# Queries of the memory heads: a fourth column group in other heads' input products, kept in memory until they are used

## The chip, the cores and the metric

The kernel runs on one core of a Trainium2 chip. Times are device microseconds (us) of one execution. Several runs of the same program were timed; the profile is of one further execution, with the hardware profiler attached. In the tables of the profile PE is the matrix engine (PEld its weight loads), DVE the vector engine, ACT the scalar engine, POOL the general engine, and SP the engine that only issues transfers here.

## The reference

Two decoder layers over 1024 tokens of width 1024, in float32. Each layer normalises its input, multiplies it with one wide input matrix, cuts the columns into branches, and adds the product of the gated branch outputs with an output matrix. Both layers have a branch that reads 256 memory tokens with 4 heads of width 128:

```python
def memory_cross_attention(q, mem, mem_g, w_mem_kv, q_g, k_g):
    mk, mv = jnp.split(rms_norm(mem, mem_g) @ w_mem_kv, 2, axis=-1)
    q = rms_norm(q.reshape(bsz, seq, X_HEADS, X_DIM), q_g)
    mk = rms_norm(mk.reshape(bsz, m, X_HEADS, X_DIM), k_g)
    s = jnp.einsum('bshd,bmhd->bhsm', q, mk).astype(jnp.float32) * (X_DIM ** -0.5)
    p = jax.nn.softmax(s, axis=-1).astype(mv.dtype)
    o = jnp.einsum('bhsm,bmhd->bshd', p, mv)
...
proj = u @ w_in
aq, ak, av, az, bh, bc, bb, bz, xq, xz = jnp.split(proj, cuts, axis=-1)
yx = memory_cross_attention(xq, mem, mem_g, w_mem_kv, x_qn, x_kn)
y = jnp.concatenate([ya * silu(az), yb * silu(bz), yx * silu(xz)], axis=-1)
return h + y @ w_out
```

Layer 0 has, beside it, differential attention (8 heads) and a short gated convolution; layer 1 has forgetting attention (12 heads). The change concerns `xq`, the queries of the memory heads: 512 columns of the input product in each layer.

## The kernel before

The normalised input `u` lies on chip, transposed, as a high and a low part. Every large product is made of three: high times high, high times low, low times high. Two kinds of product use it.

- `token_unit` (L213) takes eight blocks of 128 tokens, one after the other. For one block it makes 8 x 3 = 24 matmuls (L224 to L226); the token block is the stationary operand and the weight columns (`wqh`, `wql`) are the moving one, so the width of the moving operand is the number of weight columns. A head's query, key and value columns are one unit 384 wide (`qkv_unit`, L480; 396 wide for the first head of layer 1, with the forget columns).
- `feature_unit` (L242) has 128 weight columns stationary and 512 tokens moving, in two halves of 24 matmuls each (L257 to L259). It makes the gates (`gate_unit`, L264) and the convolution's parts.

After a block of a token unit, `post` copies the product out of its PSUM bank on ACT (`evac`, L283), and `qk_norm` (L288) normalises it: squares on ACT into a scratch tile `sq` (L292), sums on DVE (L294), a power on POOL (`rstd`, L119 to L124), and a multiplication on DVE (L297). After every second block, two blocks later, `qk_transpose` (L300) turns the queries and keys on PE in a bank of their own.

The order of the program is head by head: the head's token unit, its gates, its attention, and in layer 0 half of a convolution group. Behind the last head come the two pairs of memory heads, `x_pair` (L614) for pair 0 and pair 1. A pair loads the keys and values of the memory from `xm` (L622, written near the start of the kernel), makes a token unit of its own for the queries of both heads, 256 wide (L630), makes two gates (`xgate`, L636), and runs the attention of both heads, alternating between them over four groups of 256 tokens (L641 to L644, `x_attend` L646). Pair 1 also starts to load the output matrix (`out_early`, L752). The output product follows (`out_proj`, L791).

A planner (the Tile framework) turns this program into one fixed instruction stream for each engine, and each engine works through its stream in order. The planner may issue a later part of the program before an earlier one: blocks under `high_priority` go ahead of others where they are ready, attention (4000) and the evacuation of products (8000) among them. So the token unit of the next head runs on PE between the matmuls of the attention of the one before. What holds the planner back, beside data, is buffers. Each tile is asked for by a tag with a fixed number of buffers. Those that matter here:

- `d`, 3 PSUM banks: products of token units, of gates and of the convolution, the transposes of L303, and most of the output product
- `y`, 2 buffers: results of an attention group (L476, L560), and in layer 0 also the squares `osq` of its normalisation (L563)
- `E2`, 2 buffers: scratch of the attention, and the two `xgate` tiles of a pair
- `hs`, 3 buffers: `th` of the gates (L279) and the memory tiles `xr` (L621), among others
- `qr`, 4 buffers 384 or 396 wide, and `sq`, 1 buffer: only for the evacuation and its squares
- `yr`, 4 buffers 512 wide: only for the loads of the output product (L774)

Of the kernel before, what the change touches and what calls it, by code (L numbers as in the profile page):

```python
# [7 lines left out]
F32 = mybir.dt.float32  # L8
# [7 lines left out]
P = 128  # L16
# [17 lines left out]
class Trunk:  # L34
    def __init__(self, ctx, tc, io):
        self.tc, self.nc, self.io = tc, tc.nc, io
        nc = self.nc
        self.const = ctx.enter_context(tc.tile_pool(name="const", bufs=1))
        self.up = ctx.enter_context(tc.tile_pool(name="up", bufs=1))
        self.pa = ctx.enter_context(tc.tile_pool(name="pa", bufs=1))  # L40
        self.pk = ctx.enter_context(tc.tile_pool(name="pk", bufs=1))
        self.st = ctx.enter_context(tc.tile_pool(name="st", bufs=4))
        self.ps = ctx.enter_context(tc.tile_pool(name="ps", bufs=2, space=PSUM))
        self.dr = ctx.enter_context(tc.tile_pool(name="dr", bufs=1, space=DRAM))

# [16 lines left out]
        self.wq_n, self.e1b, self.ptb = 384, 3, 2  # L62

# [133 lines left out]
    def unit_weights(self, w, groups, lo_eng=None, ahead=None):  # L197

        nc = self.nc
        n = sum(c for _, c in groups)  # L200
        wh, wl, raws = ahead or ([], [], {})
        per = 2 if 2 * n <= 512 else 1
        for k0 in range(len(wh), KC, per):
            raw = raws[k0] if k0 in raws else self.raw_columns(w, groups, k0, per)
            for i in range(per):
                hi = self.pw.tile([P, self.wq_n], F32R, name="wqh", tag="wqh", bufs=8)
                lo = self.pw.tile([P, self.wq_n], F32R, name="wql", tag="wql", bufs=8)
                self.split(hi[:, :n], lo[:, :n], raw[:, i, :], lo_eng[(k0 + i) % len(lo_eng)] if lo_eng else nc.gpsimd)
                wh.append(hi[:, :n])
                wl.append(lo[:, :n])  # L210
        return wh, wl
# [65 lines left out]
    def gate_half(self, out, ps):  # L277
# [3 lines left out]
        nc.vector.scalar_tensor_tensor(out=out, in0=th, scalar=1.0, in1=ps, op0=ALU.add, op1=ALU.mult)  # L281

    def evac(self, ps, n):  # L283
        raw = self.p1.tile([P, self.wq_n], F32, name="qr", tag="qr", bufs=4)
        self.nc.scalar.activation(out=raw[:, :n], in_=ps[:, :n], func=AF.Copy)  # L285
        return raw

    def qk_norm(self, x, ng, gs):  # L288

        nc = self.nc  # L290
        sq = self.p1.tile([P, 256], F32, name="sq", tag="sq", bufs=1)
        nc.scalar.activation(out=sq, in_=x[:, :256], func=AF.Square, scale=float(gs) ** -0.5)  # L292
# [74 lines left out]
    def mem_kv(self, layer, um, w):  # L367
# [111 lines left out]

    def qkv_unit(self, w, cols, ng, gs, g, extra=None, pairs=False, weights=None):  # L480
        nc = self.nc
# [16 lines left out]
        if weights is None:  # L498
            weights = self.unit_weights(w, [(c, P) for c in cols] + ([] if extra is None else [extra[0]]), None if extra is None else (nc.vector, nc.gpsimd),
                                        None if extra is None else self.ahead)  # L500
        self.token_unit(weights, self.u_lhs(0), self.u_lhs(1), NB, post)
        return (qh, ql), (kh, kd, kl, kz) if pairs else (kh, kl), *[(lambda kb, v=v: v[kb // 4][:, kb % 4 * P:(kb % 4 + 1) * P]) for v in (vh, vl)]


# [16 lines left out]
    def diff_head(self, h, w, weights=None, between=None):  # L521
        qt, kt, vh, vl = self.qkv_unit(w, self.diff_cols(h), 4, 64, self.g_a, pairs=True, weights=weights)

# [89 lines left out]

    def x_pair(self, layer, pr, w, cq, cz, w_out):  # L614
        nc = self.nc
        q0h, q0l, q1h, q1l = self.att_tiles("qh", "ql", "kh", "kl")
        qns, mem = [], []
        g = self.g_x[layer]
# [6 lines left out]

        def post(tb, ps):
            qns.append(self.qk_norm(self.evac(ps, 256), 2, P))
# [69 lines left out]
    def fox_head(self, h, w):  # L697
        nc = self.nc
        extra = None
        if h == 0:  # L700
# [4 lines left out]
            extra = ((6144, 12), post_f)  # L705
        q, k, vh, vl = self.qkv_unit(w, [h * P, 1536 + h * P, 3072 + h * P], 2, P, self.g_c, extra)
        gate = self.gate_unit(w, 4608 + h * P)
# [132 lines left out]
    def run(self, out):  # L840
        nc, tc, io = self.nc, self.tc, self.io
        mem = io["mem"][0]
        with tc.tile_pool(name="p1_0", bufs=1, reuse_waits="tile") as self.p1, tc.tile_pool(name="pw_0", bufs=1, reuse_waits="tile") as self.pw:
# [37 lines left out]
            for pr in range(2):  # L881
                self.x_pair(0, pr, w, 6144, 6656, io["e_w_out"][0])
        self.out_proj(0, io["e_w_out"][0], io["x"][0], self.h_dr, io["o_norm_g"],
                      lambda: self.weights_ahead(io["o_w_in"][0], [(c, P) for c in (0, 1536, 3072)] + [(6144, 12)]))
        with tc.tile_pool(name="pw_1", bufs=1, reuse_waits="tile") as self.pw, tc.tile_pool(name="p1_1", bufs=1, reuse_waits="tile") as self.p1:
            self.wq_n, self.e1b, self.ptb = 396, 3, 3
            w = io["o_w_in"][0]
# [3 lines left out]
            for pr in range(2):  # L891
                self.x_pair(1, pr, w, 6156, 6668, io["o_w_out"][0])
        self.out_proj(1, io["o_w_out"][0], self.h_dr, out, None)
# [31 lines left out]
```

## Time and profile before

| | |
|---|---|
| three timed runs, median | 2206.74 us (2204.52 to 2206.93) |
| the profiled execution, its own time | 2204.26 us |
| its span, from the first to the last instruction | 2202.2 us |
| mean granted clock of PE | 0.996 |
| DVE busy | 1240.5 us (56% of the span) |
| ACT busy | 1053.2 us (48%) |
| POOL busy | 1020.3 us (46%) |
| transfers | 182.99 MB, mean 83 GB/s |

The busy time of PE is a sum of matmuls that overlap, with modelled ends, so what one matmul costs is read from the distance between starts in a stretch without gaps. Rows of a timeline have the start in the span, the duration, the engine, the line, the operation, and output from input with shapes. Rows of the windows have, for a stretch, its length and then for each engine the busy time in it with the number of instructions in brackets; then come the granted clock, the share of the transfer engines and GB/s. Rows of the groups have the count, busy time, mean duration of one in ns, and the idle time of the engine just before.

### The profile page before, as it was taken

What the parts mean: (1) busy time and instruction counts of PE and PEld (TensorE: products, weight loads), DVE (VectorE), ACT (ScalarE), POOL (GpSimd) and SP (SyncE); (2) the same over time, 40 slices, a digit from 0 to 9 for tenths busy, and PEclk for the clock granted to TensorE, in tenths of its full rate; (3) what the DMA queues carried; (4) which work ended last, traced back from release to release, by engine and by line L of the source; (5) the groups of instructions that cost most, each with busy time, mean ns of one, the idle gap of its engine ahead of it and who ended that gap; (6) DMA issues with size and microseconds to landing.
All of it is one profiled execution on the core that took longest, in us unless ns stands there. A gap on an engine that the chain in (4) does not pass through costs nothing.

```text
span 2202.2 us, 35113 instructions
## 1 busy us (share of the span) xinstructions
PE 2167.8 (98%) x12528; PEld 1968.7 (89%) x12528; DVE 1240.5 (56%) x2864; ACT 1053.2 (48%) x2503; POOL 1020.3 (46%) x1352
## 2 busy tenths in 40 slices
PE   8999999999999999999999999999999999999999
PEld 7889889899898899778889999999999999998887
DVE  5656756665674677654445554554545555566532
ACT  6656455464554555433334444444444444455321
POOL 5565555555555454342334555544555554522100
PEclk9999999999999999999999999999999999999999
DMA  5450210211202112387521222201122220223743
GB/s 163 138 156 19 62 52 19 73 34 47 61 29 58 37 54 88 116 270 216 187 63 35 58 58 59 63 23 53 48 56 68 58 62 25 65 73 113 232 132 102
DMA packets 216983, 182.99 MB, mean 83 GB/s; under 512 B 19516, under 2 KB 174300, under 8 KB 216808
## 3 DMA queue, kind: packets, MB, share of 16 engines
q1 hardware_dynamic: 193768, 138.80, 21.6%
q10 hardware_dynamic: 23040, 41.95, 6.2%
q8 instruction: 98, 1.61, 0.3%
q14 instruction: 77, 0.63, 0.1%
HBM read 153.32 MB, written 27.38 MB: 82 GB/s over the span
## 4 chain that ended last, share of the span: by engine, by line
PE 91%; DMA 4%; DVE 1%; POOL 1%; ACT 1%; issue 1%; SPq 0%; ACTq 0%; POOLq 0%; DVEq 0%
PE pd L225 11%; PE pd L224 11%; PE pd L226 11%; PE pss L417 8%; PE pd L258 7%; PE pd L257 7%; PE pd L259 7%; PE pd L788 5%; PE pd L786 5%; PE pd L787 5%; PE pt L451 4%; PE po L466 2%; PE po L465 2%; PE po L464 2%; PE pt L306 1%; DMA wraw<-in_e_w_out_dram 1%
## 5 line engine op out<-in xcount | busy, mean ns | idle before, releaser
L224 PE MATMUL pd<-wqh,u 128*128 128x384 f32 (+2 forms) x1504 | 502.2, 335 | 0.7 <-ACT u L130 0.7
L225 PE MATMUL pd<-wql,u 128*128 128x384 f32 (+2 forms) x1504 | 500.8, 333 | 0.1
L226 PE MATMUL pd<-wqh,u 128*128 128x384 f32 (+2 forms) x1504 | 500.8, 333 | 0.0
L225 PEld LDWEIGHTS pd<-wql,u 128*128 128x128 f32 x1504 | 284.2, 189 | 5.8 <-DVE wql L131 0.6
L224 PEld LDWEIGHTS pd<-wqh,u 128*128 128x128 f32 x1504 | 284.1, 189 | 4.8 <-ACT u L130 1.1
L226 PEld LDWEIGHTS pd<-wqh,u 128*128 128x128 f32 x1504 | 283.7, 189 | 4.7 <-DVE u L131 0.2
L257 PE MATMUL pd<-u,wfh 128*128 128x512 f32 x704 | 279.0, 397 | 0.0
L258 PE MATMUL pd<-u,wfl 128*128 128x512 f32 x704 | 278.7, 396 | 0.0
L259 PE MATMUL pd<-u,wfh 128*128 128x512 f32 x704 | 277.8, 395 | 0.0
L131 POOL TENSOR_TENSOR wql<-raw,wqh 128x384 fp32r<-128x384 f32 (+2 forms) x214 | 210.2, 998 | 78.2 <-ACT wqh L130 73.5
L285 ACT ACTIVATE qr<-pd 128x384 f32<-128x384 f32 (+2 forms) x200 | 92.9, 468 | 199.4 <-PE pd L226 198.4
L131 DVE TENSOR_TENSOR yl<-yr,yh 128x512 fp32r<-128x512 f32 x128 | 103.7, 810 | 142.3 <-ACT yh L130 134.2
L124 POOL TENSOR_TENSOR rs_r<-rs_v,neghalf 128x2 f32<-128x2 f32 (+2 forms) x220 | 176.4, 802 | 12.8
L130 ACT ACTIVATE yh<-yr 128x512 fp32r<-128x512 f32 x128 | 80.5, 630 | 207.8 <-PE pd L787 113.4
L130 ACT ACTIVATE pth<-pt 128x512 fp32r<-128x512 f32 (+1 forms) x232 | 121.8, 554 | 112.5 <-PE pt L451 107.4
L131 POOL TENSOR_TENSOR vl<-qr,vh 128x128 fp32r<-128x128 f32 x160 | 79.0, 499 | 206.4 <-ACT vh L130 205.5
L723 POOL TENSOR_TENSOR fbias<-ck,cqn 128x896 f32<-128x896 f32 (+3 forms) x96 | 112.4, 1171 | 131.8 <-DVE mx L434 109.1
L297 DVE TENSOR_TENSOR qr<-qr,rs_r 128x256 f32<-128x256 f32 x200 | 123.5, 618 | 79.8 <-POOL rs_r L124 78.6
L131 POOL TENSOR_TENSOR wfl<-rawf,wfh 128x512 fp32r<-128x512 f32 x88 | 119.6, 1362 | 102.7 <-ACT wfh L130 100.2
L130 ACT ACTIVATE wqh<-raw 128x384 fp32r<-128x384 f32 (+2 forms) x252 | 114.7, 483 | 109.5 <-DMA raw<-in_e_w_in_dram 61.2
L131 DVE TENSOR_TENSOR ptl<-pt,pth 128x512 fp32r<-128x512 f32 (+1 forms) x232 | 143.8, 639 | 34.6 <-ACT pth L130 32.2
L259 PEld LDWEIGHTS pd<-u,wfh 128*128 128x128 f32 x704 | 132.7, 188 | 27.1 <-issue 1.1
(286 smaller groups left out, 5077.5 us busy)
## 6 DMA issues: line engine op xcount, KB each, us to landing
yr<-y_dr ACTq DMA_DIRECT2D x128, 256.0 KB
raw<-in_o_w_in_dram SPq DMA_DIRECT2D x96, 192.0 KB
rawf<-in_e_w_in_dram SPq DMA_DIRECT2D x56, 256.0 KB
y_dr<-y SPq DMA_DIRECT2D x112, 128.0 KB
raw<-in_e_w_in_dram SPq DMA_DIRECT2D x64, 192.0 KB
wraw<-in_e_w_out_dram SPq DMA_DIRECT2D x32, 256.0 KB
rn<-on_dr ACTq DMA_DIRECT2D x32, 256.0 KB
rawf<-in_o_w_in_dram SPq DMA_DIRECT2D x32, 256.0 KB
```

What stands on the lines that cost most here:

```text
L124: nc.gpsimd.tensor_tensor(out=r[:, :n], in0=v[:, :n], in1=self.neghalf[:, :n], op=ALU.pow)
L130: nc.scalar.activation(out=hi, in_=src, func=AF.Copy)
L131: lo_eng.tensor_tensor(out=lo, in0=src, in1=f32(hi), op=ALU.subtract)
L224: nc.tensor.matmul(ps[:, :n], lhsT=ah(k), rhs=h, start=(k == 0), stop=False)
L225: nc.tensor.matmul(ps[:, :n], lhsT=ah(k), rhs=l, start=False, stop=False)
L226: mm = nc.tensor.matmul(ps[:, :n], lhsT=al(k), rhs=h, start=False, stop=(k == KC - 1))
L257: nc.tensor.matmul(ps, lhsT=h, rhs=uh[:, k, :], start=(k == 0), stop=False)
L258: nc.tensor.matmul(ps, lhsT=l, rhs=uh[:, k, :], start=False, stop=False)
L259: nc.tensor.matmul(ps, lhsT=h, rhs=ul[:, k, :], start=False, stop=(k == KC - 1))
L297: nc.vector.tensor_tensor(out=v, in0=v, in1=r.unsqueeze(2).broadcast_to([P, ng, gs]), op=ALU.mult)
L417: nc.tensor.matmul(ps, lhsT=q[qb // 4][rows, qs], rhs=k[c0 // 512][rows, ks], start=(i == 0), stop=(i == n - 1))
L723: nc.gpsimd.tensor_tensor(out=b[:, :kext], in0=ck[:, :kext], in1=self.cqn[:, qb, h:h + 1].broadcast_to([P, kext]), op=ALU.subtract)
```

## The change

The token unit of `x_pair` is gone. Of each layer, the heads 2 to 5 get a fourth group of 128 weight columns in their token unit, the query columns of memory head 0 to 3, so that these eight units are 512 wide and not 384. The wider block is copied out of PSUM, its last 128 columns are sent to memory (`xq_dr`) by a transfer that ACT issues, and `x_pair` loads the queries of its two heads back, two token blocks to a tile, normalises them, and transposes them, before it makes its gates. The weight tiles are 512 wide for all units. The evacuated blocks, and the tiles into which `x_pair` loads, are buffers of tag `yr`, shared with the output product; tags `qr` and `sq` are gone. The squares of a token unit go into the first 256 columns of the unit's own PSUM bank, already copied out; the squares of `x_pair` go into buffers of tag `y`. The code of `x_pair` up to its gates is traced in program order without a raised priority, where the `post` of the token unit had one.

```diff
+        self.xq_dr = [[self.dr.tile([NB, P, 2, P], F32, name=f"xq_dr{i}_{j}") for j in range(2)] for i in range(2)]
...
-                hi = self.pw.tile([P, self.wq_n], F32R, name="wqh", tag="wqh", bufs=8)
-                lo = self.pw.tile([P, self.wq_n], F32R, name="wql", tag="wql", bufs=8)
+                hi = self.pw.tile([P, 512], F32R, name="wqh", tag="wqh", bufs=8)
+                lo = self.pw.tile([P, 512], F32R, name="wql", tag="wql", bufs=8)
...
+    def evac_tile(self):
+        return self.pk.tile([P, 512], F32, name="qr", tag="yr", bufs=4)
+
     def evac(self, ps, n):
-        raw = self.p1.tile([P, self.wq_n], F32, name="qr", tag="qr", bufs=4)
+        raw = self.evac_tile()
...
-    def qk_norm(self, x, ng, gs):
-        sq = self.p1.tile([P, 256], F32, name="sq", tag="sq", bufs=1)
+    def qk_norm(self, x, ng, gs, ps=None):
+        sq = self.pa.tile([P, 256], F32, name="sq", tag="y", bufs=2) if ps is None else ps[:, :256]
...
         def post(tb, ps):
-            raw = self.evac(ps, 384 if extra is None else 396)
-            qns.append(self.qk_norm(raw, ng, gs))
+            raw = self.evac(ps, n)
+            if xq is not None:
+                layer, head = xq[0]
+                nc.scalar.dma_start(out=self.xq_dr[layer][head // 2][tb, :, head % 2, :], in_=raw[:, 384:])
+            qns.append(self.qk_norm(raw, ng, gs, ps))
...
+    def xq_cols(layer, h, c0):
+        return ((layer, h - 2), c0 + (h - 2) * P) if 2 <= h < 6 else None
...
-        def post(tb, ps):
-            qns.append(self.qk_norm(self.evac(ps, 256), 2, P))
-            if tb % 2:
-                self.later(DEFER, lambda: self.qk_transpose(qns[tb - 1:tb + 1], [(q0h, q0l, g), (q1h, q1l, g)], (tb - 1) * P))
-        self.token_unit(self.unit_weights(w, [(cq + pr * 256, 256)]), self.u_lhs(0), self.u_lhs(1), NB, post)
+        for tb in range(0, NB, 2):
+            t = self.evac_tile()
+            nc.sync.dma_start(out=t.rearrange("p (b c) -> p b c", b=2), in_=self.xq_dr[layer][pr][tb:tb + 2].rearrange("b p s c -> p b (s c)"))
+            qns = [self.qk_norm(t[:, i * 256:(i + 1) * 256], 2, P) for i in range(2)]
+            self.qk_transpose(qns, [(q0h, q0l, g), (q1h, q1l, g)], tb * P)
```

More of the change, by code (lines that the diff above doesn't have):

```diff
@@ L61, in __init__ @@
         self.attb, self.gorder = 3, (3, 2, 1, 0)
-        self.wq_n, self.e1b, self.ptb = 384, 3, 2
+        self.e1b, self.ptb = 3, 2
     def params(self, first):
@@ L388, in post_k @@
             def post_k(b, ps, pr=pr, qns=qns):
-                qns.append(self.qk_norm(self.evac(ps, 256), 2, P))
+                qns.append(self.qk_norm(self.evac(ps, 256), 2, P, ps))
                 if b == 1:
@@ L478, in gated_y, with qkv_unit @@
         self.emit_y(layer, chunk, 2 * g, y)
-    def qkv_unit(self, w, cols, ng, gs, g, extra=None, pairs=False, weights=None):
+    def qkv_unit(self, w, cols, ng, gs, g, extra=None, pairs=False, weights=None, xq=None):
         nc = self.nc
@@ L498, in qkv_unit @@
         if weights is None:
-            weights = self.unit_weights(w, [(c, P) for c in cols] + ([] if extra is None else [extra[0]]), None if extra is None else (nc.vector, nc.gpsimd),
+            weights = self.unit_weights(w, [(c, P) for c in cols] + ([] if extra is None else [extra[0]]) + ([] if xq is None else [(xq[1], P)]), None if extra is None else (nc.vector, nc.gpsimd),
                                         None if extra is None else self.ahead)
+        n = weights[0][0].shape[1]
         self.token_unit(weights, self.u_lhs(0), self.u_lhs(1), NB, post)
         return (qh, ql), (kh, kd, kl, kz) if pairs else (kh, kl), *[(lambda kb, v=v: v[kb // 4][:, kb % 4 * P:(kb % 4 + 1) * P]) for v in (vh, vl)]
+    @staticmethod
+    def xq_cols(layer, h, c0):
+        return ((layer, h - 2), c0 + (h - 2) * P) if 2 <= h < 6 else None
     def lam_setup(self):
@@ L521, in diff_head @@
     def diff_head(self, h, w, weights=None, between=None):
-        qt, kt, vh, vl = self.qkv_unit(w, self.diff_cols(h), 4, 64, self.g_a, pairs=True, weights=weights)
+        qt, kt, vh, vl = self.qkv_unit(w, self.diff_cols(h), 4, 64, self.g_a, pairs=True, weights=weights, xq=self.xq_cols(0, h, 6144))
         full = slice(0, P)
@@ L611, in conv_group, with x_pair @@
         yield
-    def x_pair(self, layer, pr, w, cq, cz, w_out):
+    def x_pair(self, layer, pr, w, cz, w_out):
         nc = self.nc
         q0h, q0l, q1h, q1l = self.att_tiles("qh", "ql", "kh", "kl")
-        qns, mem = [], []
+        mem = []
         g = self.g_x[layer]
@@ L624, in x_pair @@
             mem.append((xh, xl))
-        def post(tb, ps):
-            qns.append(self.qk_norm(self.evac(ps, 256), 2, P))
-            if tb % 2:
-                self.later(DEFER, lambda: self.qk_transpose(qns[tb - 1:tb + 1], [(q0h, q0l, g), (q1h, q1l, g)], (tb - 1) * P))
-        self.token_unit(self.unit_weights(w, [(cq + pr * 256, 256)]), self.u_lhs(0), self.u_lhs(1), NB, post)
+        for tb in range(0, NB, 2):
[3 more added lines that the diff above has]
+            self.qk_transpose(qns, [(q0h, q0l, g), (q1h, q1l, g)], tb * P)
         heads = []
@@ L705, in fox_head @@
             extra = ((6144, 12), post_f)
-        q, k, vh, vl = self.qkv_unit(w, [h * P, 1536 + h * P, 3072 + h * P], 2, P, self.g_c, extra)
+        q, k, vh, vl = self.qkv_unit(w, [h * P, 1536 + h * P, 3072 + h * P], 2, P, self.g_c, extra, xq=self.xq_cols(1, h, 6156))
         gate = self.gate_unit(w, 4608 + h * P)
@@ L881, in run @@
             for pr in range(2):
-                self.x_pair(0, pr, w, 6144, 6656, io["e_w_out"][0])
+                self.x_pair(0, pr, w, 6656, io["e_w_out"][0])
         self.out_proj(0, io["e_w_out"][0], io["x"][0], self.h_dr, io["o_norm_g"],
@@ L885, in run @@
         with tc.tile_pool(name="pw_1", bufs=1, reuse_waits="tile") as self.pw, tc.tile_pool(name="p1_1", bufs=1, reuse_waits="tile") as self.p1:
-            self.wq_n, self.e1b, self.ptb = 396, 3, 3
+            self.e1b, self.ptb = 3, 3
             w = io["o_w_in"][0]
@@ L891, in run @@
             for pr in range(2):
-                self.x_pair(1, pr, w, 6156, 6668, io["o_w_out"][0])
+                self.x_pair(1, pr, w, 6668, io["o_w_out"][0])
         self.out_proj(1, io["o_w_out"][0], self.h_dr, out, None)
```

## The prediction

> **What bounds the kernel now.** I read the page first, engines and chain of waits, and then windows over the two stretches in which the memory heads run: from the first 256-wide product of pair 0 to the last gate product of pair 1 in layer 0, and from the last gate of head 11 to the same point in layer 1.
>
> ```profile
> span 2202.2 us, 35113 instructions
> PE 2167.8 (98%) x12528; PEld 1968.7 (89%) x12528; DVE 1240.5 (56%) x2864; ACT 1053.2 (48%) x2503; POOL 1020.3 (46%) x1352
> PE 91%; DMA 4%; DVE 1%; POOL 1%; ACT 1%; issue 1%; SPq 0%; ACTq 0%; POOLq 0%; DVEq 0%
> ...
> 783.40:910.00 126.60, 126.48 (x911) 118.37 (x910) 85.88 (x236) 70.24 (x194) 49.53 (x65) 1.00 0.21 62
> 1879.50:2017.00 137.50, 137.50 (x965) 127.73 (x964) 92.78 (x245) 74.61 (x193) 49.24 (x68) 1.00 0.20 59
> ```
>
> PE sets the end: 91% of the chain is matmuls. In the memory heads' stretches too it never rests (126.48 of 126.60 us, 137.50 of 137.50). DVE, the third busy time of a window's row, works 68% of them (85.88 of 126.6; 92.78 of 137.5). So the question is twofold: how much PE work the change removes in all, and whether PE stays without gaps in these stretches when work is taken out of them.
>
> **The products: what PE gains.** The price of a matmul is the distance of starts in a gapless stretch. These are the first and last of 8 matmuls 256 wide, of 23 that are 384 wide, and of 16 with 512 moving columns.
>
> ```profile
> 794.06 0.28 PE L224 MATMUL pd<-wqh,u 128*128 128x256 f32 x1
> 794.89 0.28 PE L225 MATMUL pd<-wql,u 128*128 128x256 f32 x1
> ...
> 1478.01 0.34 PE L225 MATMUL pd<-wql,u 128*128 128x384 f32 x1
> 1481.89 0.34 PE L226 MATMUL pd<-wqh,u 128*128 128x384 f32 x1
> ...
> 838.45 0.39 PE L257 MATMUL pd<-u,wfh 128*128 128x512 f32 x1
> 841.85 0.39 PE L257 MATMUL pd<-u,wfh 128*128 128x512 f32 x1
> ```
>
> That is 0.83/7 = 0.1186 us, 3.88/22 = 0.1764 us and 3.40/15 = 0.2267 us. Removed: 4 units x 8 blocks x 24 = 768 matmuls, 91.1 us. Added: 8 units x 8 x 24 = 1536 matmuls that get 0.0503 us longer, 77.3 us. Net 13.8 us of 2204, because fewer matmuls carry the same columns. The Trainium skill (TensorE: Matmul & The Clock Gate, Back-to-back issue gap) speaks against even that: it gives N/2.4 + 2.5 ns for a warm stream, which at these widths would make 83.8 us removed and 81.9 added, 1.9 us net. The three distances here lie up to 14 ns above that formula, and the measured ones decide.
>
> The 77.3 us go into heads where PE is the chain, so they are paid in full. The 91.1 us come out of the two stretches, 45.5 us each, and are won only as far as something else doesn't take their place.
>
> **What holds the rest of the stretch.** Buffers of one tag seem to be handed out in the order in which the code asks for them, not as they come free. Witness the memory tiles `xr` (tag `hs`): the code asks for them right after the `th` tiles of the gates before.
>
> ```profile
> 141.72 0.91 SPq L383 DMA_DIRECT2D xm<-mkt  x2
> ...
> 1815.55 0.60 ACT L280 ACTIVATE th<-pd 128x512 f32<-128x512 f32 x1 [2.09 <-PE pd L259]
> 1879.27 0.94 SPq L622 DMA_DIRECT2D xr<-xm  x2
> 1879.55 0.60 ACT L280 ACTIVATE th<-pd 128x512 f32<-128x512 f32 x1 [2.09 <-PE pd L259]
> ...
> 849.14 0.99 SPq L622 DMA_DIRECT2D xr<-xm  x2
> 851.68 0.58 ACT L280 ACTIVATE th<-pd 128x512 f32<-128x512 f32 x1
> ```
>
> Their data is in memory from 142 us on. They are loaded at 849 and 1879 us, within 3 us of the last `th` asked for before them, although the three `hs` buffers stood nearly empty before. Read so, the change ties two knots. The squares of `x_pair` now ask for `y`, behind every `y` and `osq` of the attention before: pair 0 can't normalise until the last head's attention is at its last group, pair 1 until pair 0's is. And the four transposes of `x_pair` ask for banks of tag `d` ahead of its gates, so the gate products, the only other PE work of a pair, wait for the eighth normalised block. The removed token unit was what PE did meanwhile; its own squares had a buffer to themselves.
>
> So each layer's stretch becomes a chain of six steps. Their rows: the last `y` of the head before, the last gate of pair 0, its second and eighth result, in layer 0 and then in layer 1.
>
> ```profile
> 848.21 0.48 DVE L561 SCALAR_TENSOR_TENSOR y<-po,g_o,gate 128x256 f32<-128x256 f32 x1 [2.36 <-PE po L466]
> 852.41 0.68 DVE L281 SCALAR_TENSOR_TENSOR xgate<-th,pd 128x512 f32<-128x512 f32 x1
> 862.29 0.41 DVE L477 SCALAR_TENSOR_TENSOR y<-po,xgate 128x256 f32<-128x256 f32 x1
> 883.06 0.42 DVE L477 SCALAR_TENSOR_TENSOR y<-po,xgate 128x256 f32<-128x256 f32 x1
> ...
> 1937.23 0.42 DVE L477 SCALAR_TENSOR_TENSOR y<-po,gate 128x256 f32<-128x256 f32 x1 [0.25 <-PE po L466]
> 1953.63 0.41 DVE L477 SCALAR_TENSOR_TENSOR y<-po,xgate 128x256 f32<-128x256 f32 x1
> 1975.91 0.41 DVE L477 SCALAR_TENSOR_TENSOR y<-po,xgate 128x256 f32<-128x256 f32 x1
> ...
> 783.40:848.70 65.30, 65.18 (x461) 60.31 (x460) 42.99 (x118) 36.45 (x99) 31.25 (x40) 1.00 0.19 55
> 1880.20:1937.70 57.50, 57.50 (x417) 54.12 (x417) 37.27 (x104) 30.15 (x76) 27.69 (x41) 1.00 0.19 52
> ```
>
> ```profile
> L124 POOL TENSOR_TENSOR rs_r<-rs_v,neghalf 128x2 f32<-128x2 f32 x136 | 98.4, 724 | 6.3
> L122 POOL TENSOR_SCALAR rs_v<-qk_ms 128x2 f32<-128x2 f32 x136 | 34.0, 250 | 139.6 <-DVE qk_ms L294 131.9
> L294 DVE TENSOR_REDUCE qk_ms<-sq 128x2 f32<-128x256 f32 x136 | 56.7, 417 | 99.3 <-ACT sq L292 98.3
> L297 DVE TENSOR_TENSOR qr<-qr,rs_r 128x256 f32<-128x256 f32 x8 | 3.6, 448 | 5.0 <-POOL rs_r L124 5.0
> L314 DVE SCALAR_TENSOR_TENSOR ql<-pt,g_c,qh 128x256 fp32r<-128x256 f32 x48 | 23.0, 478 | 19.0 <-ACT qh L313 18.8
> L654 DVE TENSOR_REDUCE nm<-pss 128x1 f32<-128x256 f32 x64 | 25.9, 418 | 11.3 <-PE pss L417 11.0
> L659 DVE TENSOR_SCALAR ex<-ex,rl 128x256 f32<-128x256 f32 x64 | 23.5, 370 | 1.9
> L658 DVE RECIPROCAL rl<-ls 128x1 f32<-128x1 f32 x64 | 10.1, 159 | 12.9 <-ACT ex L656 12.2
> L131 DVE TENSOR_TENSOR ptl<-pt,pth 128x512 fp32r<-128x512 f32 x152 | 101.2, 685 | 17.0 <-ACT pth L130 14.9
> ```
>
> 1. The rest of the last head's attention took 65.3 and 57.5 us beside token unit and gates, with DVE busy 43.0 and 37.3. Of that, norms and their transposes are 8 x (0.417 + 0.448 + 0.478) = 10.7 us, gates 3 and 2 x 0.68, and early memory-head softmaxes 7 and 4 x (0.418 + 0.370 + 0.159): 19 and 16 us that aren't this attention's. It keeps 24 and 21 us on DVE, the lower ends; the old lengths are the upper. DVE was 66% busy then; with PE out of its way I take 72%: 33 and 30 us.
> 2. Eight norms, paced by POOL: 8 x (0.250 + 0.724) = 7.8 us, and some 2 us for the first square and the last multiplication and transposes: 10 us. Nothing runs on PE but transposes.
> 3. The four gate halves: 96 x 0.2267 = 21.8 us, with about 5 us of the pair's first scores, transposes and products between: 27 us.
> 4. The second head's first result needs the fourth half, and there is one `po` bank; six results follow. They took 20.8 and 22.3 us with other work on DVE; DVE's own share is 6 x (0.685 + 0.42) and some 6 softmaxes of 0.947, 12.3 us. I take 17.
> 5. The norms of pair 1: 10 us again.
> 6. Its gates: 27 us.
>
> Layer 0: 33 + 10 + 27 + 17 + 10 + 27 = 124 us against 126.6; layer 1: 30 + 91 = 121 against 137.5. About 19 us are recovered of the 91.1.
>
> **What else it costs.** PE will have gaps of many us, and the trace shows what follows one: after a window with PE 1.59 of 4 us busy the granted clock is 0.50 for two windows.
>
> ```profile
> 916.00:920.00 4.00, 1.59 (x10) 1.11 (x8) 2.58 (x3) 2.57 (x5) 2.55 (x2) 0.96 0.63 201
> 920.00:924.00 4.00, 2.14 (x8) 1.88 (x9) 1.86 (x5) 1.57 (x3) 0.71 (x1) 0.50 0.78 273
> 924.00:928.00 4.00, 3.07 (x12) 2.08 (x10) 3.35 (x4) 2.32 (x5) 4.00 (x4) 0.50 0.93 243
> ```
>
> Four gate stages restart after such a gap; each loses between nothing and 4 us (8 us at half clock). I take 2 us in all, since transposes come before the gates. The Trainium skill (TensorE: Matmul & The Clock Gate, Part 1) has half clock after an idle window of about 3.4 us and full clock after 3.4 busy ones; by it the four would lose 7 us.
>
> At nothing I cost: the 64 transfers out and 16 in (4.2 MB each way, transfers 20% busy here; the stores sit on ACT's queue, the loads on SP's behind `y` stores, and pair 0's can go while the last head still runs); the wider evacuation, split and weight loads, under PE's 24 x 0.2267 = 5.4 us per block; and the squares in the bank, which hold it about 0.8 us longer (one square and one sum), covered by the next block's 24 x 0.1764 = 4.2 us. If that cover fails, 160 blocks x 0.8 = 128 us would be the end, but two more banks stand ready, and I take 0. A gain is excluded there, as PE didn't wait for `d`. After the last gate, `u` comes free and the output product starts in the same order as before.
>
> **The sum.** 2204.3 + 77.3 - 19 + 2 = 2265 us for the profiled execution; the median of the runs shown lies 2.5 us above its own time, so some 2268.
>
> **The rivals.** *The gates run ahead* (buffers are not handed out in order, or the planner finds other work). Then steps 2 and 5 vanish behind gates, and DVE's 85.9 and 92.8 us at 85% set the stretches: 101 and 109 us, 54 us recovered, 2204.3 + 77.3 - 53.6 + 2.5 = 2230. For it: the old order of attention and products was mixed finely everywhere. Against it: the `xr` loads. *PE stays the bound*, the other side: if also DVE's work packs so that PE has under 6.9 us of gaps per layer, the 13.8 us come through: 2193. For it: DVE 68% busy. Against it: what is left for PE is 126.6 - 45.5 = 81 and 92 us, and DVE alone needs 86 and 93. By the formula of the skill above this rival would end at 2205, no change. *The tail doesn't shrink*: step 1 keeps its old length, because the fixed streams make the attention wait as it does now: up to 32 and 26 us more, towards 2325.
>
> **Chances.** Forecast 0.60; gates ahead 0.17; PE the bound 0.12 (with it 0.03 for no change); tail kept 0.08. The range leaves out the two cases at or below no change (0.15) and the far end of the last (0.05): 2213 to 2300. A measurement here can tell about 0.2%, 4.4 us, from no change. Faster 0.12, same 0.03, slower 0.85.
>
> **What would show it.** Right: eight units of 512-wide products at 0.227 us; PE gaps of 10 us and more before each pair's gates, with the clock at 0.5 in them; squares of `x_pair` only after the last `y` or `osq`; gate products only after the fourth pair of transposes. Wrong: gate products of a pair between matmuls of the attention before it, or an unbroken PE in the stretches.

## The result and the profile after

| | before | after |
|---|---|---|
| median | 2205.01 us (2203.34 to 2206.93, 6 runs) | 2304.85 us (2303.35 to 2308.69, 6 runs) |
| ratio to before | 1 | 1.0455, 95% interval 1.0444 to 1.0465 |
| profiled execution | 2204.26 us, span 2202.2 | 2307.14 us, span 2305.1 |
| mean granted clock | 0.996 | 0.975 |

The change makes the kernel 100 us slower. The forecast was 2268 us, 63 slower; the range ended at 2300. The direction was right, the size was not.

These are lines of the page of after: busy times, PE's busy tenths and granted clock in 40 slices, and the chain by engine.

```profile
PE 2211.8 (96%) x11760; PEld 1921.3 (83%) x11760; DVE 1234.7 (54%) x2864; ACT 1048.1 (45%) x2439; POOL 1008.9 (44%) x1320
PE   8999999999999988899999999999999999889999
PEclk9999999999999998799999999999999999988999
PE 82%; DMA 5%; DVE 4%; POOL 4%; ACT 3%; issue 2%; SPq 0%; ACTq 0%; POOLq 0%; DVEq 0%
```

Two things stand there. PE has 768 matmuls fewer and is still busy 44 us longer (2211.8 against 2167.8), though the forecast had it 14 us lighter. And it now has gaps: in slices 15 to 17 and 35 to 36 of 57.6 us each, which hold the memory heads' stretches, it falls to 8 tenths, and its clock to 7 or 8 in slices 16 and 17, 36 and 37. Its share of the chain went from 91 to 82%.

The windows over these stretches say how large the gaps are. First the two rows of before, from the first 256-wide product of pair 0 (in layer 1 from the last gate of head 11) to the last gate product of pair 1; then those of after between the same points, the start of layer 0's moved by the shift of the heads ahead of it. Length, PE, PEld, DVE, ACT, POOL, then the clock.

```profile
783.40:916.76 133.36, 133.24 (x946) 124.18 (x945) 90.88 (x246) 75.50 (x206) 53.01 (x68) 1.00 0.22 65
1880.20:2014.90 134.70, 134.70 (x948) 125.28 (x948) 90.95 (x244) 72.77 (x190) 47.55 (x67) 1.00 0.19 58
```

```profile
831.00:975.43 144.43, 113.39 (x560) 92.39 (x559) 89.30 (x236) 67.29 (x174) 49.43 (x61) 0.80 0.21 63
1987.00:2116.18 129.18, 105.54 (x544) 86.96 (x543) 84.38 (x228) 61.88 (x155) 43.94 (x59) 0.87 0.23 66
```

PE has 386 and 404 instructions fewer there, yet layer 0's stretch is 11 us longer and layer 1's only 5.5 us shorter. PE rests 31 and 24 us there, and runs at 0.80 and 0.87 of its clock. All that was taken out of the stretches is given back.

The shift of the heads comes from the last gates of head 7 and head 11, in before (first fence) and in after.

```profile
764.26 0.69 DVE L281 SCALAR_TENSOR_TENSOR gate<-th,pd 128x512 f32<-128x512 f32 x1
1880.18 0.69 DVE L281 SCALAR_TENSOR_TENSOR gate<-th,pd 128x512 f32<-128x512 f32 x1 [4.18 <-ACT th L280]
```

```profile
811.68 0.69 DVE L282 SCALAR_TENSOR_TENSOR gate<-th,pd 128x512 f32<-128x512 f32 x1
1986.98 0.68 DVE L282 SCALAR_TENSOR_TENSOR gate<-th,pd 128x512 f32<-128x512 f32 x1
```

Layer 0's heads are late by 47.4 us at the end of the last, where 38.6 were forecast, half of 77.3. By the end of layer 1's heads it is 106.8.

The last rows of after are the knots themselves, a timeline of the stretch, layer 0 and then layer 1: the last `y` of the head before, the first square of `x_pair`, the first and last gate product of pair 0, its last `y`, and the first and last gate product of pair 1.

```profile
871.75 0.48 DVE L575 SCALAR_TENSOR_TENSOR y<-po,g_o,gate 128x256 f32<-128x256 f32 x1 [2.31 <-PE po L471]
874.09 0.42 ACT L297 ACTIVATE sq<-qr 128x256 f32<-128x256 f32 x1 [0.94 <-DMA y_dr<-y]
887.77 0.40 PE L258 MATMUL pd<-u,wfh 128*128 128x512 f32 x1
916.11 0.40 PE L260 MATMUL pd<-u,wfh 128*128 128x512 f32 x1
932.50 0.42 DVE L482 SCALAR_TENSOR_TENSOR y<-po,xgate 128x256 f32<-128x256 f32 x1 [1.80 <-PE po L471]
946.01 0.77 PE L258 MATMUL pd<-u,wfh 128*128 128x512 f32 x1
947.43 0.63 PE L258 MATMUL pd<-u,wfh 128*128 128x512 f32 x1
948.66 0.39 PE L258 MATMUL pd<-u,wfh 128*128 128x512 f32 x1
975.43 0.40 PE L260 MATMUL pd<-u,wfh 128*128 128x512 f32 x1
...
2015.17 0.42 DVE L482 SCALAR_TENSOR_TENSOR y<-po,gate 128x256 f32<-128x256 f32 x1 [0.76 <-PE po L471]
2028.48 0.78 PE L258 MATMUL pd<-u,wfh 128*128 128x512 f32 x1
2058.67 0.39 PE L260 MATMUL pd<-u,wfh 128*128 128x512 f32 x1
2073.41 0.42 DVE L482 SCALAR_TENSOR_TENSOR y<-po,xgate 128x256 f32<-128x256 f32 x1 [1.14 <-PE po L471]
2087.39 0.78 PE L258 MATMUL pd<-u,wfh 128*128 128x512 f32 x1
2116.18 0.39 PE L260 MATMUL pd<-u,wfh 128*128 128x512 f32 x1
```

Read it downwards: `y`, square, gates, `y`, gates, in strict turns. The square names what it waited for, `DMA y_dr<-y`: its buffer comes free when the transfer that sends the last `y` away has landed.

### The profile page after: what moved, and what is told of

It reads as the page before. It is cut to its first block, busy times and chain, and to the rows that moved or that the text cites. A ratio compares the mean times of both kernels' runs of the same rounds, so it can differ in the third digit from the quotient of the medians.

```text
span 2305.1 us, 33833 instructions
## 1 busy us (share of the span) xinstructions
PE 2211.8 (96%) x11760; PEld 1921.3 (83%) x11760; DVE 1234.7 (54%) x2864; ACT 1048.1 (45%) x2439; POOL 1008.9 (44%) x1320
## 4 chain that ended last, share of the span: by engine, by line
PE 82%; DMA 5%; DVE 4%; POOL 4%; ACT 3%; issue 2%; SPq 0%; ACTq 0%; POOLq 0%; DVEq 0%
PE pd L226 11%; PE pd L225 11%; PE pd L227 11%; PE pss L422 6%; PE pd L258 6%; PE pd L259 6%; PE pd L260 5%; PE pd L802 4%; PE pd L800 4%; PE pd L801 4%; PE pt L456 4%; PE po L471 2%; PE po L470 2%; PE po L469 2%; DMA raw<-in_e_w_in_dram 2%
## 5 line engine op out<-in xcount | busy, mean ns | idle before, releaser
L225 PE MATMUL pd<-wqh,u 128*128 128x384 f32 (+2 forms) x1248 | 458.0, 368 | 1.5 <-ACT u L131 0.9
L226 PE MATMUL pd<-wql,u 128*128 128x384 f32 (+2 forms) x1248 | 457.5, 367 | 0.1
L227 PE MATMUL pd<-wqh,u 128*128 128x384 f32 (+2 forms) x1248 | 456.5, 366 | 0.0
L225 PEld LDWEIGHTS pd<-wqh,u 128*128 128x128 f32 x1248 | 235.8, 189 | 24.6 <-ACT u L131 1.4
L226 PEld LDWEIGHTS pd<-wql,u 128*128 128x128 f32 x1248 | 235.8, 189 | 22.8 <-DVE wql L132 0.6
L227 PEld LDWEIGHTS pd<-wqh,u 128*128 128x128 f32 x1248 | 235.5, 189 | 22.9 <-DVE u L132 0.2
L132 POOL TENSOR_TENSOR wql<-raw,wqh 128x384 fp32r<-128x384 f32 (+3 forms) x182 | 203.3, 1131 | 87.7 <-ACT wqh L131 78.6
L290 ACT ACTIVATE qr<-pd 128x384 f32<-128x384 f32 (+3 forms) x168 | 87.5, 524 | 210.8 <-PE pd L227 189.9
L132 DVE TENSOR_TENSOR yl<-yr,yh 128x512 fp32r<-128x512 f32 x128 | 98.9, 773 | 144.0 <-ACT yh L131 135.4
L131 ACT ACTIVATE wqh<-raw 128x384 fp32r<-128x384 f32 (+3 forms) x220 | 110.0, 522 | 117.2 <-DMA raw<-in_e_w_in_dram 67.5
```

The source lines that it names most:

```text
L131: nc.scalar.activation(out=hi, in_=src, func=AF.Copy)
L132: lo_eng.tensor_tensor(out=lo, in0=src, in1=f32(hi), op=ALU.subtract)
L225: nc.tensor.matmul(ps[:, :n], lhsT=ah(k), rhs=h, start=(k == 0), stop=False)
L226: nc.tensor.matmul(ps[:, :n], lhsT=ah(k), rhs=l, start=False, stop=False)
L227: mm = nc.tensor.matmul(ps[:, :n], lhsT=al(k), rhs=h, start=False, stop=(k == KC - 1))
```

## The experiments

**First question: which half of the change costs what?** Three kernels take it apart.

*Buffers alone.* No fourth group, and `x_pair` has its own token unit again.

```diff
-        return ((layer, h - 2), c0 + (h - 2) * P) if 2 <= h < 6 else None
+        return ((layer, h - 2), c0 + (h - 2) * P) if False else None
...
-        for tb in range(0, NB, 2):
-            t = self.evac_tile()
...
+        def post(tb, ps):
+            qns.append(self.qk_norm(self.evac(ps, 256), 2, P, ps))
...
+        self.token_unit(self.unit_weights(w, [((6144, 6156)[layer] + pr * 256, 256)]), self.u_lhs(0), self.u_lhs(1), NB, post)
```

> Squares in the bank, evictions in yr, 512-wide weight tiles, and nothing else of the change. Theory: these cost nothing, 2205 +- 4 us. Rival: banks held longer or shared buffers stall the heads, 2215 us or more.

Measured: 2204.09 us (2200.18 to 2205.7, 10 runs), ratio 0.9998, 0.9988 to 1.0007. Squares in the bank, evacuations in `yr` and weight tiles 512 wide cost nothing that shows. The products here are 384 wide as before, so this says nothing of a wider evacuation.

*Heads alone.* The own token unit of `x_pair` is put back as above, and the fourth group stays.

> The heads carry the fourth column group and store it, and x_pair keeps its own token unit and doesn't read it: the price of the heads alone. If PE pays the measured spacing of 512-wide token products (0.2344 us against 0.1764 at 384, 1536 times), the time is 2205 + 89 = 2294 us. If my forecast's 0.2267 holds, 2205 + 77 = 2282. If something else in the heads (banks held for the squares, shared buffers, the stores) takes part, over 2300.

Measured: 2298.7 us (2296.93 to 2300.18, 4 runs), ratio 1.0429, 1.0413 to 1.0444. The fourth group costs 94 us. PE is busy 90 us longer than before (2257.8 against 2167.8). The spacing of wide products is the larger part of the price. In layer 1, from the last gate of head 1 to that of head 5, this kernel takes 299.96 us (1292.14 to 1592.10) and buffers alone 254.71 (1239.39 to 1494.10). The four wide heads cost 45.3 us there; 768 times the longer spacing of 0.0578 us is 44.4, and 38.6 were forecast. Over both layers some 5 us beyond the 89 stay unplaced.

*Stretch alone.* No fourth group; the loads of `x_pair` read rows of `x` and not the queries.

```diff
-            nc.sync.dma_start(out=t..., in_=self.xq_dr[layer][pr][tb:tb + 2].rearrange("b p s c -> p b (s c)"))
+            nc.sync.dma_start(out=t..., in_=self.x_in[0, tb * P:(tb + 2) * P, pr * 256:(pr + 1) * 256].rearrange("(b p) c -> p b c", b=2))
```

> No fourth group in the heads; x_pair loads other data of the same size (rows of x) in place of the queries: the stretches alone. If the two orders of tags starve PE as in the changed kernel, the stretches and what follows give 2205 + 10 = 2215 us (2210 to 2222). My forecast had 2205 - 19 + 2 = 2188. If waiting for the stored queries is what costs there, this kernel gets near 2205 - 91 = 2114.

Measured: 2209.06 us (2204.51 to 2210.4, 10 runs), ratio 1.002, 1.0011 to 1.0029. PE has 91 us less to do in these stretches, and the kernel is 4 us slower. PE's busy time falls by 47.7 us only (2120.1 against 2167.8), while its mean granted clock falls to 0.974. With the 90 us of the heads that makes 42 of the 44 us by which PE is busier in after. It isn't the queries' way through memory, since the rows of `x` are there from the start. The timeline shows the same wait, the square behind the last `y` and its landing:

```profile
822.76 0.48 DVE L575 SCALAR_TENSOR_TENSOR y<-po,g_o,gate 128x256 f32<-128x256 f32 x1 [2.31 <-PE po L471]
825.09 0.42 ACT L297 ACTIVATE sq<-qr 128x256 f32<-128x256 f32 x1 [0.93 <-DMA y_dr<-y]
```

94 + 4 = 98 us, against 100 measured for the whole: the two halves add up.

**Second question: which order starves PE in the stretch?**

*Own squares.* One line, the tag of `x_pair`'s squares.

```diff
-        sq = self.pa.tile([P, 256], F32, name="sq", tag="y", bufs=2) if ps is None else ps[:, :256]
+        sq = self.pa.tile([P, 512], F32, name="sq", tag="raw", bufs=4)[:, :256] if ps is None else ps[:, :256]
```

> The changed kernel, with the squares of x_pair in buffers of tag raw, which no attention uses, in place of tag y. Theory (squares wait for the y of the attention before): squares of pair 0 start more than 20 us before the last y of the head before, the norms (16 us in layer 0) leave the chain and the gates of pair 0 run beside the last head's attention: 2235 to 2270 us. Rival (another tag, such as E2 of the gates or the queries' own buffers, or DVE, holds the stretch anyway): 2295 us or more.

Measured: 2240.12 us (2238.26 to 2242.56, 4 runs), ratio 1.016, 1.0143 to 1.0178. One tag was worth 65 us. (`raw` also has four buffers where `y` has two, and the 65 us hold that too.) Its timeline has the first square, the first and last gates of pair 0, and head 7's last `y`:

```profile
795.90 0.42 ACT L297 ACTIVATE sq<-qr 128x256 f32<-128x256 f32 x1
875.98 1.27 DVE L282 SCALAR_TENSOR_TENSOR xgate<-th,pd 128x512 f32<-128x512 f32 x2
886.03 0.69 DVE L282 SCALAR_TENSOR_TENSOR xgate<-th,pd 128x512 f32<-128x512 f32 x1 [0.17 <-ACT th L281]
887.84 0.48 DVE L575 SCALAR_TENSOR_TENSOR y<-po,g_o,gate 128x256 f32<-128x256 f32 x1
```

The square now runs 92 us ahead of the last `y`, where it came 2.3 us behind. The gates moved ahead of it too, but by 2 to 12 us only.

*Gates first.* The loads, norms and transposes of `x_pair` move behind the loop that asks for its gates; the squares keep tag `y`.

> The changed kernel, with x_pair's gates asked for ahead of its loads, norms and transposes; the squares still ask for y. Theory (transposes hold the d banks): the gates run beside the rest of the attention before, but the norms still wait for its last y, so 27 us in pair 0 and 10 us in pair 1 leave the chain of each layer, less what runs into each other: 2240 to 2265 us. Rival (the squares' y is the only knot that matters, or E2 holds the gates): 2290 to 2305 us.

Measured: 2283.01 us (2281.7 to 2284.03, 4 runs), ratio 1.0353, 1.0338 to 1.0369. This fits neither figure: 22 us are won, not 40 to 65. The timeline, with the last gate of pair 0, the last `y` and the first square, says why.

```profile
876.37 0.69 DVE L282 SCALAR_TENSOR_TENSOR xgate<-th,pd 128x512 f32<-128x512 f32 x1 [1.35 <-ACT th L281]
883.83 0.48 DVE L575 SCALAR_TENSOR_TENSOR y<-po,g_o,gate 128x256 f32<-128x256 f32 x1 [3.36 <-PE po L471]
886.33 0.42 ACT L297 ACTIVATE sq<-qr 128x256 f32<-128x256 f32 x1 [1.10 <-DMA y_dr<-y]
```

The gates do run before the last `y`, but late, as with own squares; and the square is still 2.5 us behind it.

*Both.*

> Squares in raw as in the run with own squares (2240.1 us), and the gates asked for first. If the order of the transposes before the gates still costs once the squares are free, this is faster: 2225 us or less. If the gates there are held by their own buffers (xgate, tag E2, behind the attention's e2: in that run its first xgate of pair 0 came at 875.98 us, 12 us before the last y of the head before at 887.8), it stays at 2240 +- 6 us.

Measured: 2250.61 us (2245.7 to 2251.78, 4 runs), ratio 1.0208, 1.0191 to 1.0225, 10 us more than own squares alone and outside both figures. Once the squares are free, the transposes' place before the gates does no harm; asking for the gates first does a little. Why it does, no run shows. What then holds the gates so late is something else.

*Own gates.* Own squares, and the gates in the weight buffers, idle after the last head's token unit, in place of `E2`, whose two buffers the attention before uses.

```diff
-            gate = self.gate_unit(w, cz + head * P, self.p1.tile([P, T], F32, name="xgate", tag="E2", bufs=2))
+            gate = self.gate_unit(w, cz + head * P, [self.pw.tile([P, 512], F32, name="xgate", tag=("wqh", "wql")[s], bufs=8) for _ in range(2)])
```

> The run with own squares (2240.1 us), and the gates of x_pair kept in the weight buffers wqh and wql, which are free after the last head's token unit, in place of E2. Theory: E2 is the third knot, its two buffers belong to the attention before until its end, so that run's gates of pair 0 came at 876 to 886 us and of pair 1 at 929 to 940, and PE had 18 of 20 us to do; with buffers of their own PE gets back most of the 32 us that were still lost: 2215 us (2208 to 2228), the floor being 2204.8 + 94 - 91 = 2208. Rival (DVE and the turns of the attention set the stretch, 75% busy there): 2234 to 2245 us.

Measured: 2226.42 us (2225.11 to 2230.74, 4 runs), ratio 1.0095, 1.0078 to 1.0113: 14 us less again. In the timeline the first gate of pair 0 comes 50 us before the last `y` of head 7, and even pair 1's first one before it:

```profile
847.29 0.68 DVE L282 SCALAR_TENSOR_TENSOR xgate<-th,pd 128x512 f32<-128x512 f32 x1
886.68 0.68 DVE L282 SCALAR_TENSOR_TENSOR xgate<-th,pd 128x512 f32<-128x512 f32 x1
897.29 0.48 DVE L575 SCALAR_TENSOR_TENSOR y<-po,g_o,gate 128x256 f32<-128x256 f32 x1
...
846.00:916.00 70.00, 62.03 (x329) 51.44 (x327) 47.81 (x116) 39.43 (x102) 28.79 (x28) 0.95 0.29 89
916.00:981.00 65.00, 59.27 (x324) 50.94 (x325) 45.06 (x105) 27.77 (x70) 15.63 (x11) 0.92 0.50 152
```

So `E2` was a third knot, which I hadn't seen. Of the 94 us that the heads pay, this kernel gets back 72; the floor of 91 isn't reached. The windows show PE resting 8.0 of 70 and 5.7 of 65 us with DVE 68 and 69% busy. What PE waits for there by name are results of DVE and ACT, 3.8 us of it for banks that DVE had still to empty (`po` 2.7, `pd` 1.1); the rest lies in the turns of the attention and the start of the output product. What share each of those has wasn't tried.

**Third question: why is a 512-wide product 0.234 us here and 0.227 there?** Before had both spacings already, in the output product of layer 0, where the stationary tiles are the same and only the moving weights differ: first and last of 72 with the weights in `u`, then of 96 with the weights in `wo`.

```profile
1008.22 0.39 PE L786 MATMUL pd<-u,yh 128*128 128x512 f32 x1
1024.31 0.39 PE L788 MATMUL pd<-u,yl 128*128 128x512 f32 x1
1024.54 0.40 PE L786 MATMUL pd<-wo,yh 128*128 128x512 f32 x1
1046.79 0.40 PE L788 MATMUL pd<-wo,yl 128*128 128x512 f32 x1
```

16.09/71 = 0.2266 and 22.25/95 = 0.2342. What differs is the place in SBUF, the on-chip memory. A trace holds no addresses; I added up the sizes of the pools in the order in which the kernel opens them. By these sums `u` lies at 2 to 66 KB of each partition, `wo` and the weight tiles `wqh`, `wql` at 128 KB or above. My first theory was the moving tile's address alone.

*Heads alone, weights low,* and *buffers alone, weights low*: the weight pool is opened right behind `u`, at 66 to 98 KB, and what lay there moves up. Eight chunks of the second output weights share its buffers.

```diff
+        self.pw = ctx.enter_context(tc.tile_pool(name="pw", bufs=1))
+        self.pk = ctx.enter_context(tc.tile_pool(name="pk", bufs=1))
         self.pa = ctx.enter_context(tc.tile_pool(name="pa", bufs=1))
-        self.pk = ctx.enter_context(tc.tile_pool(name="pk", bufs=1))
...
-            ws = [[p2.tile([P, 512], F32R, name=f"wo{p}_{c}") for p in range(2)] for c in range(16)]
+            ws = [[self.pw.tile([P, 512], F32R, name="wo", tag=("wqh", "wql")[p], bufs=8) if c < 8 else
+                   p2.tile([P, 512], F32R, name=f"wo{p}_{c}") for p in range(2)] for c in range(16)]
```

> Heads alone (2298.7 us), with the weight tiles wqh and wql, and half of the second output weights, moved to SBUF addresses of 66 to 98 KB per partition, from 128 KB and up; pa and pk go up in their place. In the changed kernel's trace 512-wide matmuls whose moving tile starts at 124 KB or less follow each other in 0.227 us, those at 128 KB and up in 0.234. Theory (the address of the moving tile sets it): the 1536 wide products get 0.0073 us shorter, 384-wide ones some 0.0045, together 2298.7 - 28 = 2271 us (2262 to 2280). Rival (it is not the address but the weights being fresh, or the unit's order): 2295 to 2302 us.

> The buffers alone (2204.1 us, no fourth group, x_pair with its own unit), with the weight tiles moved down as in the run before. Theory: 3840 products of 384 columns 0.0045 us shorter, 768 of 256 columns 0.005 shorter, 384 of the output product 0.0073 shorter: 2204 - 24 = 2180 us (2174 to 2188). Then the price of the fourth group is 2271 - 2180 = 91 us, the same as without the move. Rival: 2200 to 2208 us, no change.

Measured: 2298.68 us (2295.64 to 2303.01, 4 runs) and 2204.18 us (2202.5 to 2207.48, 10 runs). No change at all in either: the theory fell as I had put it. The trace shows that it was half right. These are the first and last of the same 20 wide token products and the same 20 feature products, in heads alone (first fence) and with the weights low (second; its lines have numbers one higher).

```profile
131.51 0.40 PE L258 MATMUL pd<-u,wfh 128*128 128x512 f32 x1
135.86 0.39 PE L259 MATMUL pd<-u,wfl 128*128 128x512 f32 x1
350.31 0.40 PE L227 MATMUL pd<-wqh,u 128*128 128x512 f32 x1
354.76 0.39 PE L225 MATMUL pd<-wqh,u 128*128 128x512 f32 x1
```

```profile
130.08 0.39 PE L259 MATMUL pd<-u,wfh 128*128 128x512 f32 x1
134.50 0.39 PE L260 MATMUL pd<-u,wfl 128*128 128x512 f32 x1
348.59 0.40 PE L228 MATMUL pd<-wqh,u 128*128 128x512 f32 x1
352.94 0.40 PE L226 MATMUL pd<-wqh,u 128*128 128x512 f32 x1
```

Token products went from 4.45/19 = 0.2342 to 4.35/19 = 0.2289 us: 1536 of them are 8 us. Feature products went from 4.35/19 = 0.2289 to 4.42/19 = 0.2326, since their stationary tiles `wfh`, `wfl` had been pushed above 130 KB: 2112 of them (three lines with 704 each) are 8 us as well. In heads alone the one could have paid for the other. But buffers alone has no wide products, and the same 20 feature products went there from 4.35/19 = 0.2289 (129.10 to 133.45 us) to 4.44/19 = 0.2337 (130.23 to 134.67 us) with nothing to pay for it, while its time stayed at 2204. So that the one paid for the other is not shown. New theory: both tiles of a matmul must lie below 128 KB.

*The same two with `pa` kept low too* (order `pw`, `pa`, `pk`): `u`, the weights and the stationary tiles all end below 128 KB.

> Heads alone (2298.7 us), with u, the weight tiles and the stationary tiles wfh, wfl all below 128 KB per partition. In the first move, the wide token products had a median of 0.227 us, but the 512-wide products of the feature units, whose stationary tiles had gone up, took 0.232 in place of 0.227. Theory (it needs both sides below): 2298.7 - 1920 x 0.0055 = 2288 us (2285 to 2292). Rival: 2296 to 2302 us.

> The buffers alone, no fourth group (2204.1 us), with the same placement. Theory: only 384 of the output products gain, as 384-wide spacing was 0.175 in either place: 2204.1 - 2.1 = 2202 us (2200 to 2204), so that the price of the fourth group is 86 us there. Rival: 2204 or more.

Measured, heads alone: 2287.85 us (2285.76 to 2293.91, 4 runs), 10.9 less, ratio to before 1.038, 1.0359 to 1.0401. Both kinds of product are now short in its timeline: the 20 feature products 4.33/19 = 0.2279 (131.27 to 135.60 us), the 20 token products 4.36/19 = 0.2295:

```profile
350.55 0.40 PE L228 MATMUL pd<-wqh,u 128*128 128x512 f32 x1
354.91 0.40 PE L226 MATMUL pd<-wqh,u 128*128 128x512 f32 x1
```

Buffers alone: 2195.15 us (2193.12 to 2198.14, 4 runs), ratio 0.9957, 0.9939 to 0.9974. That is 9 us less where 2 were expected; what the other 7 are isn't settled, and its profiled span is only 2.0 us below that of buffers alone (2196.4 against 2198.4). The price of the fourth group between these two is 92.7 us; without the move it was 94.6 (2298.7 - 2204.09), and 86 were expected. The medians are good to some 2 us each, so 8 us of wide products would have shown. The shorter spacing is shown by the rows; that it makes the 9 and 11 us is not, and this stays open.

The trace of buffers alone, all low, shows the spacing inside one product, too. The second output weights lie half in the low pool and half in the last one. These are the first of 24 matmuls with the low half, the first of the next 24 with the other half, and the last of those; the stationary tiles come from the same buffers.

```profile
1026.43 0.39 PE L803 MATMUL pd<-wo,yh 128*128 128x512 f32 x1
1031.88 0.40 PE L803 MATMUL pd<-wo,yh 128*128 128x512 f32 x1
1037.26 0.39 PE L805 MATMUL pd<-wo,yl 128*128 128x512 f32 x1
```

That is 5.45/24 = 0.2271 and 5.38/23 = 0.2339 us. But a border at 128 KB doesn't fit this run: by the sums the early output weights `we` lie at 126 to 158 KB here, and nine of them in a row (983.22 to 985.03 us) are 1.81/8 = 0.226 us apart.

*Own gates, all low.*

> The run before, with the moving tiles (weights wqh, wql, u) and the stationary ones (u, wfh, wfl and what shares their tags) all below 128 KB per partition. Theory (both sides below 128 KB give the shorter spacing): 1536 wide products and 384 of the output product some 0.0055 us shorter, 10 us less than the run before: 2205 us (2196 to 2218). Rival (placement is nothing): equal to the run before.

Measured: 2214.9 us (2211.54 to 2218.89, 5 runs), ratio 1.0047, 1.0031 to 1.0063; 11.5 us less than own gates, and the best that the fourth group gave here. Buffers alone got 9 us from the same move without a wide product, so these 11.5 can't be put down to the spacing of wide products. The kernel that beats both is the one without it, buffers alone with all low: 0.43% under before.

## Why the prediction was right or wrong

**PE's price, wrong: the first step that failed.** I took the spacing of 512 columns, 0.2267 us, from a feature unit and used it for a token unit. Those run at 0.2342 (the 20 of heads alone): 1536 x (0.2342 - 0.1764) = 89 us, not 77.3, and the whole of heads alone is 94. The row that would have told me stood in before, with the weights in `wo`. With 91.1 us removed, PE's net is then no gain but about nothing. The rival in which PE stays the bound, 2193 us, had no ground for that reason too: with the heads at 94 it could end no lower than 2205 + 94 - 91 = 2208. The formula of the Trainium skill (TensorE: Matmul & The Clock Gate, Back-to-back issue gap), N/2.4 + 2.5 ns, gives 215.8 ns at 512 columns. That section calls it the gap of an isolated matmul and has about 131 ns for a stream with weight loads, where the prediction took the formula for a stream; 0.2266 and 0.2342 us were measured, and neither figure fits.

**The knot of the squares, right.** Squares came 2.3 us behind the last `y`, and another tag alone gave 65 us. This is the main cause in the stretch.

**The knot of the transposes, half right.** The gate products did start only behind the norms (887.77 us), though ahead of the last three transposes (890.77 us). But asked for first they won 22 us with the squares in `y`, and lost 10 with the squares free. It was not a knot of its own; and I left out the gates' tag `E2`, worth 14 us.

**The chain of six steps, right in form and short in size.** In us, layer 0 and layer 1, each from the rows of after above; step 1 starts at 783.4 + 47.4 and 1880.2 + 106.8.

| step | forecast | measured |
|---|---|---|
| 1 rest of the last head's attention | 33, 30 | 41, 28 |
| 2 norms of pair 0 | 10, 10 | 16, 13 |
| 3 gates of pair 0 | 27, 27 | 28, 30 |
| 4 rest of pair 0's attention | 17, 17 | 16, 15 |
| 5 norms of pair 1 | 10, 10 | 14, 14 |
| 6 gates of pair 1 | 27, 27 | 29, 29 |
| sum | 124, 121 | 144, 129 |

The norms are the term that was mis-sized most, 57 us where I had 40. I had counted POOL's pace and little else; the first square also waits until the `y` has landed in memory (871.75 to 874.09 us), and POOL still has work of the attention before between (a power of 1.64 us at 880.68). The four gate stages are 8 us over, 3 of them the clock's, below. Layer 0's tail is 8 us over: DVE was busy 26.7 of its 40.8 us, 65%, where I had 24 us and 72%. Layer 1's came out 2 us under.

The stretches that I compared this with were misread, too. My windows ended at 910.00 and 2017.00 us, but the last gate products lie at 916.76 and 2014.90, so before spent 268 us there and not 264. After spends 5.6 us more (144.43 and 129.18). Stretch alone puts it at 4 us lost, where I had 17 won with the clock's 2 in it. With the 17 us of the heads these 21 make 38. The forecast was 37 short of the time measured, and 40 short of the change, 60 us against 100.

**The clock, right in kind.** After the gap before pair 1's gates, the first products lie (947.43 - 946.01)/3 = 0.47 and (948.66 - 947.43)/3 = 0.41 us apart, then 0.23: about 1.3 us lost at that restart. Three of the four restarts begin so (a first product of 0.77 or 0.78 us). In layer 1 five products took 2.21 us (from 2028.48) and three took 1.34 (from 2087.39), 1.1 and 0.7 us lost, so together some 3 us where I had 2. The estimate from the Trainium skill (same page, Part 1: about 3.4 us of busy time to full clock) was 7; what is measured lies between. What half clock cost the other products of the stretches isn't counted.

**Costs at nothing, in part shown.** Squares in the bank, evacuations in `yr` and wide tiles: 2204.09 against 2204.81 us. The wait for the stored queries: stretch alone, without it, loses about the same. The wider evacuation, split and weight loads and the 64 stores were not tried apart; heads alone holds them, and the 5 us that stay unplaced there may be theirs.

**The other rivals.** *Gates run ahead*, 2230: it isn't what happened, but own squares and own gates make it happen, and at 2240 and 2226 the estimate was near. That is luck in part: it had the heads at 77 us and 54 recovered, and in own gates they are 94 and 72. *The tail doesn't shrink*: layer 0's shrank to 41 us and not to 33, layer 1's did as forecast.

## What to carry to other kernels

Take a matmul's price from a row in which both operands lie where the new ones will lie, not only from one of the same shape. When work is moved out of a stretch, list for each remaining step the buffers that it asks for, and who asked for that tag last: sharing a tag with the stage before ties the two in program order, and here one tag cost 65 us that no count of instructions showed. Work that filled the waits of a slower chain is not won by being made cheaper elsewhere.

## What the hardware showed that was not expected

How fast matmuls with 512 moving columns follow each other depends on where their tiles lie in SBUF. With both tiles low they are 0.2266 to 0.2295 us apart in the rows above, with the moving tile in one of the last pools 0.2339 and 0.2342, and with the stationary tile above 130 KB 0.2326 and 0.2337. Where the border lies isn't known: 128 KB fits the first placements, but not the `we` tiles of the last. At 384 columns there is no such step: in buffers alone with all low, the first and last of 57 in a row are

```profile
47.68 0.42 PE L226 MATMUL pd<-wqh,u 128*128 128x384 f32 x1
57.48 0.34 PE L228 MATMUL pd<-wqh,u 128*128 128x384 f32 x1
```

9.80/56 = 0.1750 us, and before had 0.1764 with its weights above 128 KB by the same sums. I had expected 0.172 there. Why the place matters, and why at 512 alone, no run here shows.
